# Later stage times for the first and last attention groups, and two-tile last parts in the out projections, in a two-layer trunk on one core

## The chip, the core and the metric

The kernel runs on one core of one Trainium2 chip. The time is what the device takes for one launch, in microseconds (us); every engine of the core works through its own queue in order, and semaphores hold an instruction until what it reads is written and what it overwrites has been read. Three runs of the kernel before took 843.97, 845.14 and 845.42 us, median 845.14.

## What is computed

The reference is a trunk of two layers over 256 positions of width 2048, in float32. Layer 0 is attention with a forgetting term (32 heads of 64), layer 1 sliding-window attention (32 query heads, 4 key heads, window 128) with sinks and a partial rotation. Both take one input projection that also gives a gate, and end with an output projection that is added to x.

```python
for i in range(DEPTH):
    h = rmsnorm(x, norm_g[i])
    if i % N_MIXERS == 0:
        p = h @ fox_w_in[j]                  # q, k, v, gate (2048 each), log_f (32)
        y = fox_attention(q, k, v, log_f)    # softmax(q k / 8 + c[t] - c[s], causal) v
        w_out = fox_w_out[j]
    else:
        p = h @ swa_w_in[j]                  # q 2048, k 256, v 256, gate 2048
        y = swa_attention(q, k, v, swa_sinks[j])
        w_out = swa_w_out[j]
    y = y * jax.nn.silu(gate)
    x = x + y @ w_out
return rmsnorm(x, final_g)
```

## The kernel before, in words

Each float32 operand of a product is split into a high half (a cast to the matrix engine's 32-bit format) and a low half (what the cast lost), so one product of the reference is three products on TensorE: high by high and high by low in one matmul with 512 columns, low by high in one with 256. Weights stream from memory. `load` (L189 to L209) issues a transfer on SyncE's queue into one of three `wraw` buffers, ScalarE casts the high half (L205), VectorE subtracts to get the low half (L206), both into one of five `w` buffers. In a trace or an order, `w_4453` is one such tile: the number only tells tiles apart.

A `Unit` is 256 columns of an output, two column blocks of 128 (c = 0 and 1). Its 2048 deep sum is 16 weight tiles, taken in parts; a part of four tiles is 8 matmuls for each column block. `block(unit, p, c)` (L211 to L249) issues those of one part and one column block into the accumulator `acc` of that column block, one of four PSUM buffers. The loop at L883 to L895 walks a list of parts, the stream, and issues the part's block for c = 0 and then the previous part's block for c = 1, so that a part's weights are fetched three parts ahead (LOOK). All matmuls run on TensorE in the order of the program.

The attention is cut into stages that are hung into this stream. A counter, the clock, makes one tick for every two matmuls, and `after(steps, fn)` (L103) runs fn that many ticks later. For each group of two column blocks of queries a table such as FOX_DUE holds two pairs of numbers and a single one: for head pair 0 and head pair 1, the tick of the first query-key product `s` (its second pair of matmuls comes SECOND = 8 ticks later) and the tick at which the probabilities are transposed and copied (`t`); the single number is the tick of the products with the values. They count from the end of the group's key projection (L499). In layer 0 a head pair's products go to two PSUM buffers `ps_s`; VectorE adds the bias (L350) and takes the maximum (L336), ScalarE makes the exponentials (L293), VectorE scales them (L304). The second pair of matmuls of `s` writes a buffer that L336 must have read. The gate of a group takes three steps on ScalarE (L263 to L265) and more on VectorE.

An output projection (`out_units`, L583) is eight units. When an accumulator is complete, its consumer copies one half of it on ScalarE (L253, `low_half`), and VectorE adds that copy (L587) and then the accumulator itself (L588) to x. Only after L588 is the accumulator free. The first two units of each out projection begin while the last group's attention is still running; the order of their parts is written out in `out_stream` (L839).

Of the kernel before, what the change touches and what calls it, by code (L numbers as in the profile page):

```python
# [37 lines left out]


FOX_DUE = ((16, 44), (48, 74), 106)  # L40
FOX_FIRST = ((46, 76), (80, 108), 122)
FOX_LAST = ((14, 40), (44, 72), 88)
SWA_DUE = ((16, 40), (44, 64), 74)
SWA_LAST = ((26, 45), (30, 56), 68)

SECOND = 8
WBUFS = 5
# [7 lines left out]
def trunk(  # L55
# [45 lines left out]
    due = {}  # L101
# [149 lines left out]
    def low_half(ps):  # L251
        s = work.tile([P, S], F32, tag="row", name="half", bufs=4)
        nc.scalar.copy(s, ps[:, S : 2 * S])  # L253
        return s

    def whole(src, kind, consume, **kw):
        return Unit([(src[q], [4, 4]) for q in range(2)], kind, consume, **kw)
# [59 lines left out]
    class Pair:  # L317
# [36 lines left out]
        def s_first(self):  # L354

            rng, qb = BLK[0]
            ps = ps_s.tile([P, 512], F32, tag="S", name="ps_s")
            ps = ps.rearrange("p (h a k) -> p h a k", h=2, k=P)
            for hh in range(2):
                self.product(ps[:, hh], hh, qb, P)  # L360
            nc.vector.tensor_add(self.st[:, :, rng], ps[:, :, 1, :], self.bias[:, :, rng])  # L361
            for hh in range(2):
                self.reduce(ps[:, hh, 0, :], hh, rng, qb)
            self.soft(self.st, self.mx)
# [73 lines left out]
    ones_row, z, a = (once[0:H, i * S : (i + 1) * S] for i in range(3))  # L438
# [33 lines left out]
    class FoxGroup(Group):  # L472
# [13 lines left out]
        def k(self, c, ps):  # L486
            t = fox.tile([P, S], F32, tag="k", name="k", bufs=2)
            nc.vector.tensor_add(t, ps[:, 0:S], low_half(ps))
            nc.vector.tensor_mul(t, t, r0()[:, 0:S])
            kk = fox.tile([P, 2, 2, S], F32R, tag="kk", name="kk", bufs=2)  # L490
            for hh, (w, other) in enumerate(((TOP, BOTTOM), (BOTTOM, TOP))):
                nc.scalar.copy(kk[w, hh, 0, :], t[w, :])
                nc.scalar.copy(kk[other, hh, 0, :], t[w, :])
                high = kk[w, hh, 0, :].bitcast(F32)
                nc.vector.tensor_sub(kk[w, hh, 1, :], t[w, :], high)
                nc.vector.tensor_sub(kk[other, hh, 1, :], t[w, :], high)  # L496
            self.kT[c] = kk
            if c == 0:
                due = {0: FOX_FIRST, 7: FOX_LAST}.get(self.g, FOX_DUE)  # L499
                self.attend(2 * self.g, due, False, False)  # L500

        def v(self, c, ps):
# [16 lines left out]
        def pair(self, j):  # L519
            h0 = 4 * self.g + 2 * j  # L520

            def bias():

                assert "forgot" in state
                bc = fox.tile([P, 2, 3 * P], F32, tag="bc", name="bc")
                nc.gpsimd.dma_start(out=bc, in_=negc_d[h0 : h0 + 2, :].partition_broadcast(P))  # L526
                for hh in range(2):
                    diagonal = bc[:, hh, :].rearrange("p (b k) -> p b k", k=P)[:, 0:3:2, :]
                    filled = fill_where_not(diagonal, [[0, 2], [-1, P]], 0, 1)
                if h0 == SINK:  # L530
                    with tc.issue_after(filled.ins):
                        nc.gpsimd.dma_start(out=state["sink"], in_=sink_d.partition_broadcast(P))
                return bc

            def soft(st, mx):

                c2 = cq[:, :, h0 : h0 + 2]
                nc.vector.tensor_add(mx, mx, c2)
                nc.vector.tensor_sub(mx, c2, mx)  # L539
                normalise(st, exps(st, mx))  # L540

            def operands():
                kk = self.kT[j]
                return self.qT[j], (kk[:, 0], kk[:, 1])

            return Pair(j, operands, 1.0, soft, bias)
# [36 lines left out]
    def out_units(src, done):  # L583
        def consumer(u):
            def consume(c, ps):
                m = 2 * u + c
                nc.vector.tensor_add(xT[:, m, :], low_half(ps), xT[:, m, :])  # L587
                nc.vector.tensor_add(xT[:, m, :], ps[:, 0:S], xT[:, m, :])  # L588
                done(m)

            return consume

        first = [
            Unit(
                [(src[u, 0], [4, 4]), (src[u, 1][:, 0:4, :], [4]), (src[u, 1][:, 4:8, :], [4])],
                "wgt", consumer(u), acts=ys,
            )
            for u in range(2)
        ]
        return first + [whole(src[u], "wgt", consumer(u), acts=ys) for u in range(2, 8)]  # L600
# [115 lines left out]

    fox_units = units
    first_out = out_units(fox_out_d, to_layer1)


# [32 lines left out]
    class SwaGroup(Group):  # L753
# [6 lines left out]
        def q(self, c, ps):  # L760
# [3 lines left out]
            if c == 0:  # L764
                self.attend(2 * self.u, SWA_LAST if self.u == 7 else SWA_DUE, self.u == 7, True)

# [27 lines left out]
    for u in range(8):  # L794
        G = SwaGroup(u)
        swa_units.append(whole(swa_in_d[u], "wgt", G.q))
        swa_units.append(whole(swa_in_d[10 + u], "wgt", gate_consumer(r1, G, u == 7)))

    last_out = out_units(swa_out_d, to_end)
    last_out[7] = whole(swa_out_d[7], "tok", finish, acts=ys, halves=False)  # L800

# [34 lines left out]
    def in_turn(units):  # L836
        return [(u, p) for u in units for p in range(len(u.parts))]

    def out_stream(units):  # L839

        a, b = units[0:2]
        early = [(a, 0), (a, 1), (a, 2), (b, 0), (b, 1), (b, 2), (a, 3), (b, 3)]
        return early + in_turn(units[2:])


# [3 lines left out]
    start += [(q0, 5), (v0, 6), (v0, 7), (k0, 5), (q0, 6), (v0, 8), (k0, 6)]  # L849
    stream = (  # L850
        start + in_turn(fox_units[3:]) + out_stream(first_out) + in_turn(swa_units) + out_stream(last_out)
    )
    fetched = [0]
# [107 lines left out]
```

## Time and profile before

| | us |
|---|---|
| three runs | 843.97, 845.14, 845.42 (median 845.14) |
| profiled execution | 844.52 |
| its span | 842.5 |
| TensorE busy | 828.4 |
| VectorE busy | 669.7 |
| ScalarE busy | 545.2 |
| mean granted TensorE clock | 0.995 of full |

The profile is one execution. Busy times are sums over the engine's instructions; TensorE's instructions are pipelined, so the distance between the starts of two rows says more of its speed than the length of a row. The granted clock is the share of full speed that the chip's control gave TensorE. A bracket at a row's end is the engine's idle time ahead of it, and who ended it.

### The profile page before, as it was taken

What the parts mean: (1) busy time and instruction counts of PE and PEld (TensorE: products, weight loads), DVE (VectorE), ACT (ScalarE), POOL (GpSimd) and SP (SyncE); (2) the same over time, 40 slices, a digit from 0 to 9 for tenths busy, and PEclk for the clock granted to TensorE, in tenths of its full rate; (3) what the DMA queues carried; (4) which work ended last, traced back from release to release, by engine and by line L of the source; (5) the groups of instructions that cost most, each with busy time, mean ns of one, the idle gap of its engine ahead of it and who ended that gap; (6) DMA issues with size and microseconds to landing.
All of it is one profiled execution on the core that took longest, in us unless ns stands there. A gap on an engine that the chain in (4) does not pass through costs nothing.

```text
span 842.5 us, 13416 instructions
## 1 busy us (share of the span) xinstructions
PE 828.4 (98%) x4906; PEld 717.1 (85%) x4906; DVE 669.7 (79%) x1428; ACT 545.2 (65%) x1067; POOL 61.6 (7%) x93
## 2 busy tenths in 40 slices
PE   8999999999999999999999999999999999999996
PEld 7887888888888888888888888888888888888885
DVE  5898978879687887968677778788898889876555
ACT  6676866757576675756555555567766776666552
POOL 1020100100000010000011110000000000003211
PEclk9999999999999999999999999999999999999998
DMA  8666554646455464654465554544444435354532
GB/s 280 235 237 210 172 195 158 231 156 212 171 178 209 156 232 155 204 179 137 175 208 193 200 187 163 180 170 129 171 151 151 158 144 166 134 196 164 197 100 100
DMA packets 26385, 150.51 MB, mean 179 GB/s; under 512 B 3232, under 2 KB 5440, under 8 KB 10704
## 3 DMA queue, kind: packets, MB, share of 16 engines
q1 hardware_dynamic: 23904, 142.22, 49.2%
q0 software_dynamic: 1408, 6.36, 2.4%
q10 hardware_dynamic: 1008, 1.07, 0.4%
q8 instruction: 39, 0.64, 0.3%
q14 instruction: 26, 0.21, 0.1%
HBM read 147.50 MB, written 2.15 MB: 178 GB/s over the span
## 4 chain that ended last, share of the span: by engine, by line
PE 88%; DVE 6%; DMA 2%; ACT 2%; issue 1%; SPq 1%; DVEq 0%; ACTq 0%
PE acc L76 79%; PE ps_s L76 3%; PE psy L76 3%; PE pt L79 2%; DVE w L206 2%; DMA wraw<-in_fox_in_dram 2%; DMA wraw<-in_vf_dram 1%; ACT w L205 0%; ACT st L293 0%; DVE ssq L824 0%; SPq L200 0%; DVE q L314 0%; DVE xs L157 0%; DVE st L397 0%; DVE kk L496 0%
## 5 line engine op out<-in xcount | busy, mean ns | idle before, releaser
L76 PE MATMUL acc<-xs,w 128*128 128x256 f32 (+1 forms) x2624 | 486.4, 340 | 0.3 <-ACT w L205 0.3
L76 PEld LDWEIGHTS acc<-xs,w 128*128 128x128 f32 x2624 | 407.6, 189 | 60.7 <-issue 3.9
L206 DVE TENSOR_TENSOR w<-wraw,w 128x1024 fp32r<-128x1024 f32 (+4 forms) x275 | 323.9, 1183 | 99.3 <-ACT w L205 97.1
L205 ACT CAST w<-wraw 128x1024 fp32r<-128x1024 f32 (+4 forms) x275 | 278.3, 1016 | 146.6 <-PE acc L76 124.7
L76 PE MATMUL acc<-ys,w 128*128 128x512 f32 x960 | 170.8, 338 | 0.0
L76 PEld LDWEIGHTS acc<-ys,w 128*128 128x128 f32 x960 | 147.6, 189 | 21.6 <-issue 0.6
L76 PE MATMUL acc<-w,xs 128*128 128x256 f32 (+2 forms) x608 | 114.3, 334 | 1.3 <-ACT w L205 0.7
L76 PEld LDWEIGHTS acc<-w,xs 128*128 128x128 f32 x608 | 94.6, 189 | 14.5 <-ACT w L205 1.8
L253 ACT COPY half<-acc 128x256 f32<-128x256 f32 x112 | 41.3, 369 | 52.1 <-PE acc L76 51.3
L293 ACT ACTIVATE st<-st,mx 128x128 f32<-128x128 f32 (+1 forms) x128 | 56.7, 444 | 11.5 <-DVE mx L539 5.7
L372 ACT COPY pts<-pt 128x384 f32<-128x384 f32 x64 | 30.4, 475 | 14.1 <-PE pt L79 14.1
L76 PE MATMUL ps_s<-kk,q 128*128 128x512 f32 (+2 forms) x192 | 35.9, 307 | 3.2 <-DVE mx L336 2.4
L610 POOL TENSOR_TENSOR acc<-acc,sq 128x256 f32<-128x256 f32 x28 | 29.9, 1069 | 105.1 <-ACT sq L604 105.1
L304 DVE TENSOR_SCALAR st<-st,rl 128x128 f32<-128x128 f32 (+1 forms) x128 | 33.3, 323 | 1.0
L79 PE MATMUL pt<-ident,st 128*128 128x128 f32 x192 | 31.4, 272 | 0.0
L76 PEld LDWEIGHTS ps_s<-kk,q 128*128 128x128 f32 x192 | 26.3, 190 | 5.1 <-issue 3.6
L608 POOL COPY acc<-sq 128x256 f32<-128x256 f32 x2 | 1.9, 936 | 327.0 <-ACT sq L604 327.0
L79 PEld LDWEIGHTS pt<-ident,st 128*128 128x128 f32 x192 | 23.3, 140 | 2.5
L526 POOL DMA_DIRECT2D bc<-negc_d x16 | 8.8, 553 | 219.3 <-DVE st L361 188.3
L313 ACT CAST q<-qT 64x256 fp32r<-64x256 f32 x32 | 12.8, 401 | 18.6 <-DVE qT L734 18.2
L157 DVE SCALAR_TENSOR_TENSOR xs<-xT,g_sb,xs 128x256 fp32r<-128x256 f32 x32 | 22.0, 711 | 3.2 <-ACT xs L156 3.2
L293 ACT ACTIVATION_READ_ACCUMULATOR st<-st,mx 128x1 f32 x128 | 23.9, 187 | 0.0
(136 smaller groups left out, 590.6 us busy)
## 6 DMA issues: line engine op xcount, KB each, us to landing
wraw<-in_fox_in_dram SPq DMA_DIRECT2D x58, 1024.0 KB, 5.0
wraw<-in_swa_in_dram SPq DMA_DIRECT2D x36, 1024.0 KB, 4.9
wraw<-in_fox_out_dram SPq DMA_DIRECT2D x14, 1024.0 KB, 5.0
wraw<-in_swa_out_dram SPq DMA_DIRECT2D x14, 1024.0 KB, 4.9
bc<-negc_d POOLq DMA_DIRECT2D x16, 384.0 KB, 4.9
wraw<-in_fox_in_dram SPq DMA_DIRECT2D x4, 512.0 KB, 5.6
wraw<-in_fox_out_dram SPq DMA_DIRECT2D x4, 512.0 KB, 3.7
wraw<-in_swa_out_dram SPq DMA_DIRECT2D x4, 512.0 KB, 3.7
```

Source lines behind the costliest of these rows:

```text
L76: tc.keep_in_program_order(nc.tensor.matmul(*args, **kw))
L79: tc.keep_in_program_order(nc.tensor.transpose(out, in_, ident))
L157: nc.vector.scalar_tensor_tensor(out=xs[:, kt, 1, :], in0=xT[:, kt, :], scalar=g, in1=xs[:, kt, 0, :].bitcast(F32), op0=ALU.mult, op1=ALU. ...
L205: state["split"] = nc.scalar.copy(w[:, :, 0, :], raw)
L206: nc.vector.tensor_tensor(out=w[:, :, 1, :], in0=raw, in1=w[:, :, 0, :].bitcast(F32), op=ALU.subtract)
L253: nc.scalar.copy(s, ps[:, S : 2 * S])
L293: nc.scalar.activation(st[:, hh, rng], st[:, hh, rng], AF.Exp, bias=nm[:, qb, hh : hh + 1], accum_out=l[:, qb, hh : hh + 1],)
L304: nc.vector.tensor_scalar_mul(st[:, hh, rng], st[:, hh, rng], rl[:, qb, hh : hh + 1])
L313: nc.scalar.copy(q2[w, hh, :], t[w, :])
L372: nc.scalar.copy(group.pts[hh][:, self.j, :], pt[:, 0 : 3 * P])
L526: nc.gpsimd.dma_start(out=bc, in_=negc_d[h0 : h0 + 2, :].partition_broadcast(P))
L610: nc.gpsimd.tensor_add(sums[0], sums[0], s)
```

## The change

Group 0's stages of layer 0 (FOX_FIRST) all come 8 ticks later. Group 1 gets a table of its own, in which the first head pair comes 6 ticks later and the second 6 ticks later too, with the products with the values at the same tick. The last group of layer 0 (FOX_LAST) and of layer 1 (SWA_LAST) come 0 to 4 ticks later, the latter's first `s` at the same tick. In both out projections the first two units' parts are cut otherwise: eight tiles, four, two and two instead of eight, four and four, with the second transfer holding 6 tiles and the third 2; and the order of these two units' parts is a0 to a3, b0 to b3, a4, b4 instead of a0, a1, a2, b0, b1, b2, a3, b3.

```diff
 FOX_DUE = ((16, 44), (48, 74), 106)
-FOX_FIRST = ((46, 76), (80, 108), 122)
-FOX_LAST = ((14, 40), (44, 72), 88)
+FOX_FIRST = ((54, 84), (88, 116), 130)
+FOX_NEXT = ((22, 50), (54, 80), 106)
+FOX_LAST = ((16, 44), (48, 76), 92)
 SWA_DUE = ((16, 40), (44, 64), 74)
-SWA_LAST = ((26, 45), (30, 56), 68)
+SWA_LAST = ((26, 48), (34, 60), 72)
...
-                due = {0: FOX_FIRST, 7: FOX_LAST}.get(self.g, FOX_DUE)
+                due = {0: FOX_FIRST, 1: FOX_NEXT, 7: FOX_LAST}.get(self.g, FOX_DUE)
...
         first = [
             Unit(
-                [(src[u, 0], [4, 4]), (src[u, 1][:, 0:4, :], [4]), (src[u, 1][:, 4:8, :], [4])],
+                [(src[u, 0], [4, 4]), (src[u, 1][:, 0:6, :], [4, 2]), (src[u, 1][:, 6:8, :], [2])],
                 "wgt", consumer(u), acts=ys,
             )
             for u in range(2)
...
         a, b = units[0:2]
-        early = [(a, 0), (a, 1), (a, 2), (b, 0), (b, 1), (b, 2), (a, 3), (b, 3)]
+        early = [(u, p) for u in (a, b) for p in range(4)] + [(a, 4), (b, 4)]
         return early + in_turn(units[2:])
```

The changed file has one line more near its top, so its line numbers are one higher: the subtraction is L207, the bias addition L351, the maximum L337, the accumulator's addition L589.

The first place is VectorE at group 0's first query-key product, in the order before:

```order
L206 TENSOR_TENSOR w_743<-wraw_741,w_743 128x4x256
L350 TENSOR_TENSOR st_754<-ps_s_756,bc_698 128x256
L350 TENSOR_TENSOR st_754<-ps_s_757,bc_698 128x256
L336 ISA st_754,mx_755<-ps_s_756,st_754 128x256
L336 ISA mx_755 128x1
```

The same place in the changed kernel:

```order
L207 TENSOR_TENSOR w_743<-wraw_741,w_743 128x4x256
L207 TENSOR_TENSOR w_763<-wraw_741,w_763 128x4x256
L351 TENSOR_TENSOR st_774<-ps_s_776,bc_718 128x256
L351 TENSOR_TENSOR st_774<-ps_s_777,bc_718 128x256
L337 ISA st_774,mx_775<-ps_s_776,st_774 128x256
L337 ISA mx_775 128x1
```

A second weight subtraction, of w_763, now stands ahead of the two bias additions; before, the subtraction of that weight tile stood behind the maximum.

The second place is VectorE in layer 0's out projection, where the first unit (its accumulator for c = 0 is acc_4338 before) is consumed. Before:

```order
L206 TENSOR_TENSOR w_4466<-wraw_4464,w_4466 128x4x256
L206 TENSOR_TENSOR w_4485<-wraw_4464,w_4485 128x4x256
L587 TENSOR_TENSOR xT_82<-half_4496,xT_82 128x256
L588 TENSOR_TENSOR xT_82<-acc_4338,xT_82 128x256
L206 TENSOR_TENSOR w_4516<-wraw_4514,w_4516 128x4x256
L157 SCALAR_TENSOR_TENSOR xs_80<-xT_82,g_sb_58,xs_80 128x256
```

In the changed kernel, where that accumulator is acc_4336:

```order
L207 TENSOR_TENSOR w_4496<-wraw_4494,w_4496 128x4x256
L207 TENSOR_TENSOR w_4511<-wraw_4494,w_4511 128x4x256
L588 TENSOR_TENSOR xT_82<-half_4518,xT_82 128x256
L207 TENSOR_TENSOR w_4534<-wraw_4532,w_4534 128x4x256
L589 TENSOR_TENSOR xT_82<-acc_4336,xT_82 128x256
L207 TENSOR_TENSOR w_4563<-wraw_4532,w_4563 128x4x256
```

A weight subtraction, of w_4534, now stands between the addition of the copied half and that of the accumulator. The order in layer 1's out projection differs in the same way.

The third place is TensorE there, from the first unit's last block for c = 0 (acc_4338 and w_4422 before) to the third unit's first (acc_4556 before). Before:

```order
L76 MATMUL acc_4338<-ys_81,w_4422 128x512 x4
L76 MATMUL acc_4338<-ys_81,w_4422 128x256 x4
L76 MATMUL acc_4455<-ys_81,w_4389 128x512 x4
L76 MATMUL acc_4455<-ys_81,w_4389 128x256 x4
L76 MATMUL acc_4425<-ys_81,w_4444 128x512 x4
L76 MATMUL acc_4425<-ys_81,w_4444 128x256 x4
L76 MATMUL acc_4378<-ys_81,w_4422 128x512 x4
L76 MATMUL acc_4378<-ys_81,w_4422 128x256 x4
L76 MATMUL acc_4556<-ys_81,w_4466 128x512 x4
```

And in the changed kernel, from acc_4336 and w_4453 to acc_4566:

```order
L77 MATMUL acc_4464<-ys_81,w_4420 128x512 x4
L77 MATMUL acc_4464<-ys_81,w_4420 128x256 x4
L77 MATMUL acc_4336<-ys_81,w_4453 128x512 x2
L77 MATMUL acc_4336<-ys_81,w_4453 128x256 x2
L77 MATMUL acc_4464<-ys_81,w_4435 128x512 x2
L77 MATMUL acc_4464<-ys_81,w_4435 128x256 x2
L77 MATMUL acc_4438<-ys_81,w_4475 128x512 x2
L77 MATMUL acc_4438<-ys_81,w_4475 128x256 x2
L77 MATMUL acc_4378<-ys_81,w_4453 128x512 x2
L77 MATMUL acc_4378<-ys_81,w_4453 128x256 x2
L77 MATMUL acc_4566<-ys_81,w_4496 128x512 x4
```

Between the two stand 16 matmuls, counting the first unit's last block, where there were 32. The third unit's first accumulator takes the buffer of the first unit's for c = 0 in both kernels.

## The prediction

> **What bounds the kernel now.** I read the page first, then TensorE's waits, then the timeline of the places where it waits. The profiled execution took 844.52 us, 842.5 of them the span; the sum below is made against it. The page's first part and its chain of waits:
>
> ```profile
> PE 828.4 (98%) x4906; PEld 717.1 (85%) x4906; DVE 669.7 (79%) x1428; ACT 545.2 (65%) x1067; POOL 61.6 (7%) x93
> PE 88%; DVE 6%; DMA 2%; ACT 2%; issue 1%; SPq 1%; DVEq 0%; ACTq 0%
> ```
>
> TensorE is busy for 98% of the span and 88% of the chain is its own work. The number of products hardly depends on the change, so what it can bring or cost is TensorE's idle time, and the clock that idle time takes with it. TensorE's waits, grouped by who releases them (total us, count, longest):
>
> ```profile
> PE ps_s L76 <- DVE mx L336: 2.4, 1, 2.4
> PE acc L76 <- ACT w L205: 1.0, 2, 0.7
> PE ps_s L76 <- DVE kk L496: 0.6, 2, 0.4
> ```
>
> One wait of 2.4 us for VectorE stands out, and two small ones for the keys (`kk`). TensorE's timeline around them (start, us, operation, count, idle before it):
>
> ```profile
> 59.33 0.62 PE L76 MATMUL ps_s<-kk,q 128*128 128x512 f32 x2
> 59.79 2.94 PE L76 MATMUL acc<-xs,w 128*128 128x512 f32 x16
> 65.18 0.47 PE L76 MATMUL ps_s<-kk,q 128*128 128x256 f32 x2 [2.44 <-DVE mx L336]
> 65.49 9.63 PE L76 MATMUL acc<-xs,w 128*128 128x512 f32 x44
> 74.95 0.49 PE L79 MATMUL pt<-ident,st 128*128 128x128 f32 x3
> ...
> 80.51 7.18 PE L76 MATMUL acc<-xs,w 128*128 128x256 f32 x40
> 87.52 0.49 PE L79 MATMUL pt<-ident,st 128*128 128x128 f32 x3
> ...
> 88.33 0.40 PE L76 MATMUL ps_s<-kk,q 128*128 128x512 f32 x1
> 89.11 0.47 PE L76 MATMUL ps_s<-kk,q 128*128 128x512 f32 x1 [0.39 <-DVE kk L496]
> ```
>
> From these I take my unit: 40 products from 80.51 to 87.52 are 7.01 us, 0.1753 us each, so 16 of them (a part of four tiles, both column blocks) are 2.81 us. By that, 44 products should take 7.71 us, but from 65.49 to 74.95 they took 9.46: 1.75 us more, with no wait in them. The windows of half a microsecond say why (after the busy times, the granted clock, then DMA share and GB/s):
>
> ```profile
> 66.00:66.50 0.50, 0.50 (x3) 0.45 (x2) 0.50 (x2) 0.49 (x1) 0.00 (x0) 0.66 0.33 115
> 69.00:69.50 0.50, 0.50 (x3) 0.40 (x3) 0.50 (x1) 0.00 (x0) 0.00 (x0) 0.50 0.58 111
> 69.50:70.00 0.50, 0.50 (x5) 0.50 (x5) 0.50 (x2) 0.00 (x0) 0.00 (x0) 0.93 0.74 180
> ```
>
> The granted clock falls to 0.50 at about 66.16 (0.66 is the mean of 0.16 us at full and 0.34 at half) and is back at about 69.53: 3.4 us at half speed, 1.7 us lost. So the wait of 2.44 us cost 2.6 us of start-to-start time (62.60, where the 16 products end by my unit, to 65.18) and 1.7 us behind it.
>
> **The change, part by part.** First, group 0's stages come 8 ticks, 16 products, later. The first product (`ps_s`, two matmuls) is hung behind the 16 products that it stood ahead of; behind it come 16 others, then the pair that waits. Everything up to the pair is the same work: 59.33 + 2.81 + 0.46 (the pair's 59.33 to 59.79) + 2.81 = 65.41. VectorE's and ScalarE's rows decide whether the pair can run then:
>
> ```profile
> 62.60 1.42 DVE L206 TENSOR_TENSOR w<-wraw,w 128x1024 fp32r<-128x1024 f32 x1
> 63.95 0.74 DVE L350 TENSOR_TENSOR st<-ps_s,bc 128x256 f32<-128x256 f32 x2
> 64.61 0.41 DVE L336 CUSTOM_DVE_ANT_0 st<-ps_s,st 128x256 f32<-128x256 f32 x1
> 68.79 1.22 DVE L206 TENSOR_TENSOR w<-wraw,w 128x1024 fp32r<-128x1024 f32 x1 [0.25 <-ACT w L205]
> 69.93 0.15 DVE L539 TENSOR_TENSOR mx<-cq,mx 128x4 f32<-128x4 f32 x1
> ```
>
> ```profile
> 63.38 0.63 ACT L264 ACTIVATE gate_e<-gate_e 128x512 f32<-128x512 f32 x1
> 64.04 0.63 ACT L265 ACTIVATE gate_e<-gate_e 128x512 f32<-128x512 f32 x1
> 64.58 1.03 ACT L205 CAST w<-wraw 128x1024 fp32r<-128x1024 f32 x1
> 67.71 1.04 ACT L205 CAST w<-wraw 128x1024 fp32r<-128x1024 f32 x1 [1.07 <-PE acc L76]
> ```
>
> Later on TensorE is not simply later on VectorE: in the new order a second weight subtraction (w_763) stands ahead of the two bias additions (L350) on VectorE's queue, and its cast stands ahead of one gate step on ScalarE. The cast can start at 63.38 + 0.54 (64.04 to 64.58) = 63.92; the subtraction follows 1.08 later (67.71 to 68.79), at 65.00; the next operation 1.14 later (68.79 to 69.93), at 66.14; from the first addition to TensorE's pair are 1.23 us (63.95 to 65.18): 67.37. The pair then waits 67.37 − 65.41 = **1.96 us instead of 2.58: −0.62 us**. The wait moves with its cause. Were the subtraction not in between, the whole 2.58 would go; that is the other end. On the losing side I find nothing above the old price, since what was queued there is the same work.
>
> The clock behind it is the open price: 1.7 us if 1.96 us of idleness still lowers it, nothing if not. The trace has a fall after 2.44 us and none after the 0.78 us start-to-start at 88.33. 1.96 is nearer to 2.44; I take **no gain, 0**, with −1.7 as the other end.
>
> [...]
>
> Second, group 1's stages come 6 ticks later. At 88.33 to 89.11 its keys were late: 0.78 where a pair's first takes 0.23 (half of 0.46), 0.55 lost. 12 products more (2.1 us) ahead of it cover that, **−0.55**. Against it stands that TensorE, less held up, arrives earlier: 0.62 at most, still covered; with the dip gone too it comes 2.3 us earlier and some 0.35 remains. For the following stages of the two groups the same chaining leaves 0 to 0.5 us between what TensorE wants and what VectorE has ready, so 0, with +0.5 as the worse end.
>
> Third, the layers' last groups, 2 to 4 ticks later:
>
> ```profile
> 386.15 0.40 PE L76 MATMUL ps_s<-kk,q 128*128 128x512 f32 x1
> 386.77 0.47 PE L76 MATMUL ps_s<-kk,q 128*128 128x512 f32 x1 [0.23 <-DVE kk L496]
> ```
>
> ```profile
> 732.89 1.09 PE L76 MATMUL ps_s<-kk,q 128*128 128x128 f32 x8
> 733.82 1.57 PE L76 MATMUL acc<-xs,w 128*128 128x256 f32 x8
> 735.39 1.49 PE L76 MATMUL ps_s<-kk,q 128*128 128x128 f32 x8
> 736.72 2.04 PE L76 MATMUL acc<-xs,w 128*128 128x256 f32 x12
> ```
>
> In layer 0 the second product comes 0.62 after the first, 0.39 of it lost; the row names 0.23 as idle. I take 0.3. In layer 1 eight products took 1.33 us (735.39 to 736.72) where the same eight took 0.93 (732.89 to 733.82): 0.40. Both are covered by 4 to 8 products more: **−0.3 and −0.40**.
>
> Fourth, the out projections. Two more casts and subtractions of half size each cost nothing as long as both engines wait there, and they do (1.77 us before a cast, 1.59 before a subtraction, next fence). The two weight transfers become 768 and 256 KB instead of twice 512, in the same queue and three parts ahead: 0. The products are the same, only four last blocks are now two tiles long. That makes the distance short between the first unit's last block and the third unit's first, which takes over the first unit's accumulator. The rows, TensorE's lag to ScalarE at layer 0's end first:
>
> ```profile
> 409.01 1.64 PE L76 MATMUL acc<-w,xs 128*128 128x512 f32 x8
> 416.62 3.77 PE L76 MATMUL acc<-ys,w 128*128 128x512 f32 x19
> ```
>
> ```profile
> 409.30 0.48 ACT L372 COPY pts<-pt 128x384 f32<-128x384 f32 x1 [0.29 <-PE pt L79]
> 426.79 1.05 ACT L205 CAST w<-wraw 128x1024 fp32r<-128x1024 f32 x1 [1.77 <-PE acc L76]
> ```
>
> ```profile
> 427.88 1.23 DVE L206 TENSOR_TENSOR w<-wraw,w 128x1024 fp32r<-128x1024 f32 x1 [1.59 <-ACT w L205]
> 429.02 0.42 DVE L587 TENSOR_TENSOR xT<-half,xT 128x256 f32<-128x256 f32 x1
> ...
> 435.97 0.42 DVE L588 TENSOR_TENSOR xT<-acc,xT 128x256 f32<-128x256 f32 x1
> 436.31 1.22 DVE L206 TENSOR_TENSOR w<-wraw,w 128x1024 fp32r<-128x1024 f32 x1
> ```
>
> Let T be the start of the first unit's last block (w_4453). TensorE wants the third unit's first product (acc_4566) four blocks of four products later: T + 16 × 0.1753 = T + 2.80. That product waits for VectorE's addition of acc_4336 (L588 of before). At T the buffer of w_4420 comes free; the cast of w_4511 into it starts at T + 0.29 (the block at 409.01, the copy at 409.30), its subtraction 1.09 later (426.79 to 427.88) at 1.38, the half's addition 1.14 later at 2.52. Next on VectorE's queue is now not the accumulator's addition but the subtraction of w_4534, at 2.52 + 0.34 (435.97 to 436.31) = 2.86; its cast, freed at T + 1.40 by the block of w_4435, is ready for that, 1.40 + 0.29 + 1.09 = 2.78. The accumulator's addition starts 1.14 later, T + 4.00, ends after 0.42 at 4.42, and TensorE follows 0.16 later (65.02, the end of the L336 row, to 65.18): T + 4.58. **The new wait is 4.58 − 2.80 = 1.78 us.** Before, these four blocks were four tiles long, TensorE wanted the accumulator at T + 5.61 and no wait shows. Behind the waiting product stands everything: all matmuls run in program order. Layer 1's end has the same order on VectorE, so **+3.56** together. The ends: 1.65 if the links are 0.13 shorter together, 1.85 if the cast of w_4534 is 0.15 later than worked out; and 1.7 more for each that lowers the clock, as 2.44 us did; 1.78 is a little nearer to that than to 0.78, but 0.66 short of it, and I take none.
>
> **Sum.** 844.52 + 3.56 − 0.62 − 0.55 − 0.3 − 0.40 = 846.2 us against the profiled execution. The median of the three runs, 845.14, is 0.62 above that execution; I give half of it and forecast **846.5 us**.
>
> **The rivals.**
> *New clock falls.* The 1.78-us waits lower the clock, once or in both layers: 846.2 + 1.7 = 847.9, or 849.6. [...]
> *No fall at all.* Waits of below 2 us leave the clock alone, the old fall goes: start −2.3 (0.62 + 1.7) and 0.2 of the keys' wait instead of 0.55: 844.52 + 3.56 − 2.32 − 0.2 − 0.7 = 844.9, no change. For it: the shorter gaps of the trace left the clock at full. Against: 1.96 is 80% of 2.44. [...]
> *The out projection does not wait.* If the addition of acc_4336 ran ahead of w_4534's subtraction, or VectorE were 1.8 us earlier than my chain, only the gains stay: 844.52 − 1.87 = 842.6, and 841.0 without the fall: faster. For it: TensorE shows no wait over the whole out projection today, and VectorE idles 1.59 us there. Against: the order of VectorE's queue is fixed, and each link of the chain has its row.
>
> **How the numbers follow.** Forecast .40, new falls .27, no fall .16, no new wait .17. Changes below 0.2% (1.7 us: 843.45 to 846.83) can't be told from none here. Of the forecast, with its own spread of about 1 us and its median between 846.2 and 846.8, .25 lies within and .15 above; new falls lie above, .27; no fall lies within, .16; no new wait lies below with .15, and .02 within. So faster .15, same .43, slower .42. The range reaches down to 843.2, which leaves most of the third rival out, and up to 849.4, which leaves the double fall's upper half out. The likeliest case's own range is 845.2 to 847.4.
>
> **What would show it.** Each out projection has one wait of 1.6 to 1.9 us on `acc`, released by VectorE's accumulator addition, some 2.8 us behind the start of the first unit's last block; if none is there, the fourth part is wrong. The wait at 65 is still on the VectorE maximum (L336 of before), near 2 us, at about 65.4, with a weight subtraction just ahead of the bias additions; if it is under 0.5, my queue reading there is wrong. The windows behind all three waits show whether the clock fell: that is the price I know least. The keys' waits at 89 and 387 and the long eight products at 735 should be gone.

## The result

The changed kernel takes 846.65 us (median of 20 runs, 845.33 to 848.13), the kernel before 844.41 (20 runs, 842.98 to 845.97): a ratio of 1.0025, with a 95% interval of 1.0018 to 1.0032. So it is slower by 2.2 us, and 0.15 us off the forecast. The interval excludes no change at all; its lower end, 0.18%, just reaches below the 0.2% that the prediction takes as the least that can be told from none. The profiled execution took 845.78 us, with a span of 843.8.

TensorE's waits in the changed kernel (total us, count, longest) show the price at once:

```profile
PE acc L77 <- DVE xT L589: 3.1, 2, 1.6
PE ps_s L77 <- DVE mx L337: 1.7, 1, 1.7
...
PE pt L80 <- DVE st L305: 0.7, 1, 0.7
PE ps_s L77 <- DVE kk L497: 0.4, 1, 0.4
```

The first row is new: twice 1.57 us for VectorE's addition of an accumulator. TensorE's and VectorE's timelines at the first of the two, and ScalarE's cast of w_4511:

```profile
416.35 14.95 PE L77 MATMUL acc<-ys,w 128*128 128x512 f32 x84
432.86 12.40 PE L77 MATMUL acc<-ys,w 128*128 128x512 f32 x69 [1.57 <-DVE xT L589]
```

```profile
429.68 1.23 DVE L207 TENSOR_TENSOR w<-wraw,w 128x1024 fp32r<-128x1024 f32 x1 [0.88 <-ACT w L206]
430.82 0.42 DVE L588 TENSOR_TENSOR xT<-half,xT 128x256 f32<-128x256 f32 x1
431.16 1.22 DVE L207 TENSOR_TENSOR w<-wraw,w 128x1024 fp32r<-128x1024 f32 x1
432.29 0.42 DVE L589 TENSOR_TENSOR xT<-acc,xT 128x256 f32<-128x256 f32 x1
```

```profile
428.60 1.05 ACT L206 CAST w<-wraw 128x1024 fp32r<-128x1024 f32 x1 [1.06 <-PE acc L77]
```

With T = 428.60 − 0.29 = 428.31 the subtraction starts at T + 1.37, the half's addition at T + 2.51, the subtraction between the two at T + 2.85, the accumulator's addition at T + 3.98, TensorE at T + 4.55. It wanted the accumulator at T + 2.80 = 431.11; counted on TensorE alone, the 84 products that start at 416.35 end at 431.08, so T is right. From start to start the wait costs 1.75 us.

The start of the changed kernel, on TensorE:

```profile
62.56 2.95 PE L77 MATMUL acc<-xs,w 128*128 128x512 f32 x16
67.20 0.47 PE L77 MATMUL ps_s<-kk,q 128*128 128x256 f32 x2 [1.68 <-DVE mx L337]
67.51 8.09 PE L77 MATMUL acc<-xs,w 128*128 128x512 f32 x44
75.44 0.49 PE L80 MATMUL pt<-ident,st 128*128 128x128 f32 x3
...
88.28 0.48 PE L77 MATMUL ps_s<-kk,q 128*128 128x512 f32 x1
89.17 0.47 PE L77 MATMUL ps_s<-kk,q 128*128 128x512 f32 x1 [0.41 <-DVE kk L497]
...
111.74 1.56 PE L77 MATMUL acc<-xs,w 128*128 128x512 f32 x8
114.01 0.70 PE L80 MATMUL pt<-ident,st 128*128 128x128 f32 x3 [0.70 <-DVE st L305]
```

The wait for the maximum is 1.68 us (1.83 from start to start: 67.20 − 62.56 − 2.81). VectorE shows the second weight subtraction ahead of the bias additions, 0.18 us earlier than forecast:

```profile
64.82 1.23 DVE L207 TENSOR_TENSOR w<-wraw,w 128x1024 fp32r<-128x1024 f32 x1 [1.17 <-ACT w L206]
65.96 0.74 DVE L351 TENSOR_TENSOR st<-ps_s,bc 128x256 f32<-128x256 f32 x2
```

In this execution the clock did not fall behind it: the 44 products took 7.93 us instead of 9.46. The wait for the keys at 88 is still there, and a new one stands before the transposes at 114.

To see what each stretch gave, I compare the products with the values (`psy`), which stand once in every group. Of before, and then of the change:

```profile
125.55 1.57 PE L76 MATMUL psy<-pts,vg 128*64 128x256 f32 x16
371.93 1.57 PE L76 MATMUL psy<-pts,vg 128*64 128x256 f32 x16
415.11 1.57 PE L76 MATMUL psy<-pts,vg 128*64 128x256 f32 x16
562.53 1.52 PE L76 MATMUL psy<-pts,vs 128*64 128x512 f32 x8
751.21 1.52 PE L76 MATMUL psy<-pts,vs 128*64 128x512 f32 x8
```

```profile
124.30 1.57 PE L77 MATMUL psy<-pts,vg 128*64 128x256 f32 x16
370.72 1.57 PE L77 MATMUL psy<-pts,vg 128*64 128x256 f32 x16
414.84 1.57 PE L77 MATMUL psy<-pts,vg 128*64 128x256 f32 x16
562.61 1.52 PE L77 MATMUL psy<-pts,vs 128*64 128x512 f32 x8
752.10 1.52 PE L77 MATMUL psy<-pts,vs 128*64 128x512 f32 x8
```

By the second group the changed kernel is 1.25 us ahead, and between there and 371 nothing happens. (That 1.25 us is mostly the fall of the clock that this execution didn't have; the run of the last groups alone shows it.) At 415 and 752 the products are hung 4 ticks later than before, behind 8 products (1.40 us) more, which have to be taken off: the last group of layer 0 gained 0.46 us (−0.27 − 1.40 = −1.67 after −1.21), the out projection of layer 0 lost 1.75 (from −1.67 to +0.08), layer 1's last group gained some 0.6 (0.89 − 1.40 = −0.51 after +0.08), and the rest, to the span's +1.3, is the second out projection's loss of 1.8.

### The profile page after: what moved, and what is told of

It is laid out like the page before. It is cut to its first block, busy times and chain, and to the rows that moved or that the text cites. A ratio compares the mean times of both kernels' runs of the same rounds, so it can differ in the third digit from the quotient of the medians.

```text
span 843.8 us, 13420 instructions
## 1 busy us (share of the span) xinstructions
PE 827.5 (98%) x4906; PEld 717.1 (85%) x4906; DVE 668.6 (79%) x1432; ACT 546.2 (65%) x1071; POOL 59.9 (7%) x93
## 4 chain that ended last, share of the span: by engine, by line
PE 88%; DVE 5%; ACT 2%; DMA 2%; issue 2%; SPq 1%; DVEq 0%; ACTq 0%
PE acc L77 79%; PE ps_s L77 3%; PE psy L77 3%; PE pt L80 2%; DVE w L207 2%; DMA wraw<-in_fox_in_dram 2%; ACT w L206 1%; SPq L201 1%; ACT st L294 0%; DVE ssq L825 0%; DVE xs L158 0%; SPq L813 0%; DVE q L315 0%; DVE scaled L705 0%; DVE kk L497 0%
## 5 line engine op out<-in xcount | busy, mean ns | idle before, releaser
L207 DVE TENSOR_TENSOR w<-wraw,w 128x1024 fp32r<-128x1024 f32 (+4 forms) x279 | 324.5, 1166 | 100.7 <-ACT w L206 98.3
L77 PE MATMUL acc<-ys,w 128*128 128x512 f32 (+1 forms) x960 | 171.4, 338 | 3.1 <-DVE xT L589 3.1
L294 ACT ACTIVATE st<-st,mx 128x128 f32<-128x128 f32 (+1 forms) x128 | 56.7, 444 | 12.7 <-DVE mx L540 7.2
L294 ACT ACTIVATION_READ_ACCUMULATOR st<-st,mx 128x1 f32 x128 | 23.9, 187 | 0.0
```

Source lines behind the costliest of these rows:

```text
L77: tc.keep_in_program_order(nc.tensor.matmul(*args, **kw))
L207: nc.vector.tensor_tensor(out=w[:, :, 1, :], in0=raw, in1=w[:, :, 0, :].bitcast(F32), op=ALU.subtract)
L294: nc.scalar.activation(st[:, hh, rng], st[:, hh, rng], AF.Exp, bias=nm[:, qb, hh : hh + 1], accum_out=l[:, qb, hh : hh + 1],)
```

## The experiments

In these, line numbers are those of each run's own file and differ by one or two, and each median stands beside that of the kernel before on the same chip. Many runs share one reading, the mean granted clock of an execution: 3.4 us at half speed, as in the profile of before, are 1.7 us of 843, or 0.002 of that mean. It is a rough sign. The traces of the kernel before and of the changed one also have the clock at half in their last 4.9 and 3.9 us, where TensorE has run out of work, and that takes another 0.003 and 0.002 off the mean. In the kernel before (us, then busy times, the granted clock at 0.50, DMA share and GB/s):

```profile
838.00:840.00 2.00, 0.00 (x0) 0.00 (x0) 1.18 (x3) 0.00 (x0) 0.00 (x0) 0.50 0.92 330
```

Of the profiled executions, the two with a fall in the trace (before, and the later stage times with the out projections as before) have a mean of 0.995, the others 0.996 to 0.998. So I take a mean of 0.995 or less as a sign of a fall ahead of the end, 0.997 and more as a sign of none, and 0.996 as either; that is an estimate, and counts by 0.995 can miss some.

**One part at a time: the start alone.**

```diff
-FOX_FIRST = ((46, 76), (80, 108), 122)
+FOX_FIRST = ((54, 84), (88, 116), 130)
+FOX_NEXT = ((22, 50), (54, 80), 106)
...
-                due = {0: FOX_FIRST, 7: FOX_LAST}.get(self.g, FOX_DUE)
+                due = {0: FOX_FIRST, 1: FOX_NEXT, 7: FOX_LAST}.get(self.g, FOX_DUE)
```

> Only the stage tables of the first two groups are changed, the rest is the kernel before. My theory: the pair's wait in group 0 stays, 1.7 us idle instead of 2.4, the clock does not fall behind it, and half of that gain is given back by 115 us because VectorE is behind (a new wait of some 0.7 us before a transpose near 114): the second product with the values starts some 1.2 us earlier than in the kernel before, and the time is 1.2 us lower, 843.2 against a median of 844.4. Rival: the whole of the removed wait and clock fall stays gained, 842.1 or less. Second rival: the gain was that one execution's, whose clock did not fall by chance, and the time is that of before.

Measured: 843.42 us against 844.08, a ratio of 0.9992 (0.9983 to 1.0000). That is 0.66 us, about half of what my theory said, and the interval reaches the second rival's no change. In the trace the second `psy` stands 1.2 us earlier than before, with the wait at 114 (0.7 us) in it. But before's profiled execution had a fall of the clock and this one hadn't. Of 11 executions 1 has a mean clock of 0.995 or less; of the kernel before's, over the four comparisons, 48 of 86. Its eight executions at 0.997 and above take 843.07 to 844.12, with a median of 843.4; the eight of the kernel before at that clock on the same chip have 843.4 too. So what the start's new times gained is, by this count, fewer executions with a fall; between executions without one there is next to no gain.

**The last groups alone.**

```diff
-FOX_LAST = ((14, 40), (44, 72), 88)
+FOX_LAST = ((16, 44), (48, 76), 92)
...
-SWA_LAST = ((26, 45), (30, 56), 68)
+SWA_LAST = ((26, 48), (34, 60), 72)
```

> Only the last groups' stages are later, the rest is the kernel before. My theory: 0.5 to 0.6 us less in each layer, 844.1 - 1.0 = 843.1; the wait for the keys near 387 and the long eight products near 735 are gone. Rival: what is gained there is lost again behind it in the out projection, and the time is that of before.

Measured: 843.41 against 844.44, 0.9986 (0.9977 to 0.9995). The theory holds: 1.03 us, and none of it is given back. The two places that the prediction named are mended in the changed kernel's trace as well: no wait for the keys near 387, and the eight products from 736.70 take 0.92 us instead of 1.33.

This run's profiled execution has the old start, with a wait of 2.2 us, and no fall behind it. Its second `psy`:

```profile
124.17 1.57 PE L76 MATMUL psy<-pts,vg 128*64 128x256 f32 x16
```

That is as early as in the changed kernel (124.30). To take out what happened ahead of the attention, count from group 0's first query-key product. It starts at 59.05 here, at 59.33 in the kernel before, and in the changed kernel, 2.81 us of products later, at 62.09. The second `psy` follows after 65.12, 66.22 and 62.21 + 2.81 = 65.02 us. So against an old start without a fall the changed start gains 0.1 us; the 1.2 us against the profile of before are its fall, of whose 1.53 us (9.46 against 7.93 for the 44 products) 1.1 are left by then.

**The out projections alone.**

```diff
-                [(src[u, 0], [4, 4]), (src[u, 1][:, 0:4, :], [4]), (src[u, 1][:, 4:8, :], [4])],
+                [(src[u, 0], [4, 4]), (src[u, 1][:, 0:6, :], [4, 2]), (src[u, 1][:, 6:8, :], [2])],
...
-        early = [(a, 0), (a, 1), (a, 2), (b, 0), (b, 1), (b, 2), (a, 3), (b, 3)]
+        early = [(u, p) for u in (a, b) for p in range(4)] + [(a, 4), (b, 4)]
```

> Only the out projections' first units are cut and ordered as in the change. My theory: one wait of 1.5 to 1.6 us idle (1.75 from start to start) on the accumulator's addition in each layer and nothing else: 844.4 + 3.5 = 847.9, more where the clock falls behind them. Rival: part of the changed kernel's loss came from its last groups' stages, then this one is less than 2 us slower than the kernel before.

Measured: 847.81 against 844.08, 1.0039 (1.0027 to 1.0051), with the two waits of 1.57 us. The three parts add up: −0.66 − 1.03 + 3.73 = +2.04, against +2.24 for the whole. This run's trace held a surprise at the old start:

```profile
65.11 0.48 PE L76 MATMUL ps_s<-kk,q 128*128 128x256 f32 x2 [2.49 <-DVE mx L336]
65.42 8.09 PE L76 MATMUL acc<-xs,w 128*128 128x512 f32 x44
73.35 0.49 PE L79 MATMUL pt<-ident,st 128*128 128x128 f32 x3
```

The same wait as before, even 0.05 us longer, and the 44 products behind it take 7.93 us: no fall.

**The accumulator's wait taken away.** The third unit accumulates in the scores' two PSUM buffers, which are idle by then:

```diff
-        return first + [whole(src[u], "wgt", consumer(u), acts=ys) for u in range(2, 8)]
+        return first + [
+            whole(src[u], "wgt", consumer(u), acts=ys, acc=(ps_s, "S") if u == 2 else None)
+            for u in range(2, 8)
+        ]
```

> The changed kernel, with the third unit of each out projection accumulating in the two PSUM buffers of the scores, which are idle there, so that it does not wait for the first unit's accumulators. My theory: both waits of 1.57 us go, 1.75 us each from start to start, and no other takes their place: 846.65 - 3.5 = 843.1 us, faster than the kernel before. Rival: the weights are the cause (half-size casts and subtractions, other transfers), the waits only move to the weights of the third unit and the time stays at 846 to 847.

Measured: 843.45 against 844.08, 0.9991 (0.9982 to 0.9999), and TensorE waits for no addition in the trace. The theory holds; weights, transfers and half-size casts are not the cause. The traces say so without the spread of the times: from the `psy` at 415 to the one at 562 TensorE takes 145.96 us here, 147.77 in the changed kernel, and 145.96 in the run further below that has the same stage times and the old out projections. From the `psy` at 751 to the kernel's last products (`rows`) it is 83.75, 85.56 and 83.80. The two waits, 1.8 us each by this measure, are the whole price of the new cut.

**The two additions exchanged.**

```diff
-                nc.vector.tensor_add(xT[:, m, :], low_half(ps), xT[:, m, :])
+                half = low_half(ps)
                 nc.vector.tensor_add(xT[:, m, :], ps[:, 0:S], xT[:, m, :])
+                nc.vector.tensor_add(xT[:, m, :], half, xT[:, m, :])
```

> The changed kernel, with the two additions of an out projection's consumer in the other order: the accumulator first, the copied half second. The accumulator then comes free ahead of the weight subtraction between them, 1.14 + 0.34 us earlier. My theory: the waits go from 1.75 to 0.3 us each, 846.65 - 2.9 = 843.7 us. Rival: the accumulator's addition is held by something else than the place in VectorE's queue, and the wait stays over 1 us.

Measured: 843.15 against 844.08, 0.9992 (0.9983 to 1.0000). TensorE's row in layer 0's out projection:

```profile
415.80 24.37 PE L77 MATMUL acc<-ys,w 128*128 128x512 f32 x136
```

136 products in one row; at 0.1753 us each they are 23.84, so half a us at most is left for a wait; by the two distances used above (146.11 and 84.04 us) 0.15 and 0.24 are left, as expected. VectorE's order was the cause: with the same additions, but the accumulator's one ahead of the subtraction, the time is 3.5 us below the changed kernel's, 3.2 when each is set against the kernel before of its own comparison.

**One size changed: last parts of three tiles.**

```diff
-                [(src[u, 0], [4, 4]), (src[u, 1][:, 0:6, :], [4, 2]), (src[u, 1][:, 6:8, :], [2])],
+                [(src[u, 0], [4, 4]), (src[u, 1][:, 0:5, :], [4, 1]), (src[u, 1][:, 5:8, :], [3])],
```

> The changed kernel with the two units' last parts three tiles long instead of two (8, 4, 1 and 3 tiles). My theory: the distance from the first unit's last block to the third unit's first product is 24 products instead of 16, 4.21 us instead of 2.80, and VectorE's chain stays at 4.55: the waits go from 1.75 to some 0.35 us each, 846.65 - 2.8 = 843.9. Rival: the wait comes with the order of the parts, whatever their length, and stays over 1 us.

Measured: 844.87 against 844.44, 1.0009 (1.0000 to 1.0018), waits of 0.8 us where I expected 0.35.

```profile
433.19 17.17 PE L77 MATMUL acc<-ys,w 128*128 128x512 f32 x96 [0.83 <-DVE xT L589]
```

```profile
430.01 1.23 DVE L207 TENSOR_TENSOR w<-wraw,w 128x1024 fp32r<-128x1024 f32 x1 [0.55 <-ACT w L206]
432.63 0.42 DVE L589 TENSOR_TENSOR xT<-acc,xT 128x256 f32<-128x256 f32 x1
```

The chain is the forecast's, T + 4.55 (433.19, with T = 430.01 − 1.37 = 428.64). My count of the distance was wrong: the second unit's part between them is now one tile long, so the four blocks hold 6 + 2 + 6 + 6 = 20 products, not 24. TensorE wants the accumulator at T + 3.51, and 4.55 − 3.51 = 1.04 us from start to start is what stands there. So the wait follows the distance.

**The good parts together: later stage times, out projections as before.**

> All of the change's later stage times (first two groups and the layers' last groups), with the out projections as before. My theory: the parts add up. The last groups gave 0.46 us in layer 0 and 0.58 in layer 1 by the distances in the changed kernel, the start alone 843.4: so 842.4 us, no wait on the accumulator, faster than before by 0.2%. Rival: the last groups' stages, hung later, need the out projections' new cut to have work beside them; then a new wait stands at 409 or 747 and the time is 843.4 or more.

Measured: 842.53 against 844.44, 0.9980 (0.9971 to 0.9989), as expected, and faster than before. Its profiled execution had a fall of the clock behind a wait of only 1.85 us:

```profile
67.27 0.48 PE L77 MATMUL ps_s<-kk,q 128*128 128x256 f32 x2 [1.85 <-DVE mx L337]
67.59 9.65 PE L77 MATMUL acc<-xs,w 128*128 128x512 f32 x44
77.07 0.49 PE L80 MATMUL pt<-ident,st 128*128 128x128 f32 x3
```

```profile
66.00:68.00 2.00, 0.73 (x4) 0.66 (x5) 2.00 (x9) 0.33 (x1) 0.00 (x0) 0.90 0.63 127
68.00:70.00 2.00, 2.00 (x8) 1.71 (x7) 2.00 (x4) 0.89 (x2) 0.00 (x0) 0.50 0.92 385
70.00:72.00 2.00, 2.00 (x11) 1.73 (x11) 1.54 (x8) 1.05 (x1) 0.55 (x1) 0.74 0.41 156
```

**The start's wait covered.** By now I held that VectorE is behind until 115 us, whatever is hung where. To test it, 20 more products were put ahead of the waiting pair (on top of the last kernel):

```diff
-FOX_FIRST = ((54, 84), (88, 116), 130)
+FOX_FIRST = ((54, 94), (88, 116), 130)
...
-            after(SECOND, self.s_first)
+            after(self.second, self.s_first)
...
+            self.second = 18 if self.j == 0 and getattr(group, "g", None) == 0 else SECOND
```

> Later stage times as in the run with those alone, out projections as before, and for group 0's first head pair the second pair of matmuls hung 18 ticks behind the first instead of 8, its transposes 10 ticks later: 20 products more stand ahead of the pair that waits. My theory: VectorE is behind until some 115 us, so the 1.7-us wait at 65 goes and most of it comes back as waits near 75 to 115 on the maximum, the keys or the scaled probabilities; the second product with the values starts within 0.7 us of where it does without this, 842.4 to 841.7 us. Rival: the wait is local, all of it is gained, 840.7 us.

Measured: 842.09 against 844.44, 0.9975 (0.9966 to 0.9985), 0.44 us less than without it, which is within the intervals. TensorE at the places that wait:

```profile
79.78 0.47 PE L77 MATMUL ps_s<-kk,q 128*128 128x256 f32 x2 [0.96 <-DVE mx L337]
...
88.57 0.47 PE L77 MATMUL ps_s<-kk,q 128*128 128x512 f32 x1 [0.42 <-ACT w L206]
...
113.96 0.70 PE L80 MATMUL pt<-ident,st 128*128 128x128 f32 x3 [1.08 <-DVE st L305]
```

The wait of 1.85 us at 65 is gone. Those at 80 and 88 have come instead, and the one at 114 has grown from 0.70 to 1.08. The transposes start at 113.96, in the changed kernel at 114.01. That is what the theory says; but it is also what one late chain before those transposes would do.

**That chain's wait covered.** What is late there shows in VectorE's order of before, and then of the change, at group 1's second head pair:

```profile
109.36 0.17 DVE L538 TENSOR_TENSOR mx<-mx,cq 128x4 f32<-128x4 f32 x1
109.56 0.16 DVE L539 TENSOR_TENSOR mx<-cq,mx 128x4 f32<-128x4 f32 x1
109.74 1.23 DVE L206 TENSOR_TENSOR w<-wraw,w 128x1024 fp32r<-128x1024 f32 x1
```

```profile
110.08 0.15 DVE L539 TENSOR_TENSOR mx<-mx,cq 128x4 f32<-128x4 f32 x1
110.22 1.23 DVE L207 TENSOR_TENSOR w<-wraw,w 128x1024 fp32r<-128x1024 f32 x1
111.36 0.16 DVE L540 TENSOR_TENSOR mx<-cq,mx 128x4 f32<-128x4 f32 x1
```

A weight subtraction has slipped between two steps of 0.15 us, and the exponentials behind them start 1.8 us later (ScalarE's L294 at 111.56; L293 of before at 109.76): 1.14 for the subtraction, the rest because the first step itself stands later. Hanging the transposes 12 products later covers that; first without the edit of the last run, then with it:

```diff
-FOX_NEXT = ((22, 50), (54, 80), 106)
+FOX_NEXT = ((22, 50), (54, 86), 106)
```

> Later stage times with the out projections as before, and group 1's second head pair transposed 6 ticks (12 products, 2.1 us) later: 86 instead of 80. In the changed kernel a weight subtraction stands on VectorE between the two small steps on the maximum ahead of that pair's exponentials, which start at 111.56 instead of 109.76, and TensorE waits 0.7 us before the transposes at 114. My theory: that wait goes, 0.87 us from start to start, nothing takes its place: 842.5 - 0.85 = 841.7. Rival: VectorE is behind in its sum of work, and the wait comes back at the next product or transpose: 842.5.

> As the run with group 0's second pair of matmuls 18 ticks behind the first, and group 1's second head pair transposed 6 ticks later. My theory: the wait of 1.1 us at 114 goes, the one of 1.0 at 80 and the short one at 88 stay: 842.1 - 1.2 = 840.9. Rival, VectorE behind in its sum of work: 842.1, with the wait at another place.

Measured: 841.43 and 840.25 us, against 844.34: ratios of 0.9977 (0.9965 to 0.9989) and 0.9958 (0.9944 to 0.9972). In neither is there a wait at 114. My reading that VectorE is behind in its sum of work falls: the 1.2 us between these two runs is what covering the wait at 65 brings once the wait at 114 no longer swallows it; with that wait in place the same edit brought 0.44. The intervals of the two runs overlap by a little, but the traces agree: from the first query-key product to the second `psy` they take 61.53 and 60.43 us.

**The next wait covered too.**

```diff
-FOX_FIRST = ((54, 94), (88, 116), 130)
+FOX_FIRST = ((54, 94), (88, 122), 134)
...
-            self.second = 18 if self.j == 0 and getattr(group, "g", None) == 0 else SECOND
+            self.second = (18, 14)[self.j] if getattr(group, "g", None) == 0 else SECOND
```

> As the last one, and in group 0's second head pair too the second pair of matmuls is hung later, 14 ticks behind the first, with its transposes 6 and the products with the values 4 ticks later. My theory: the wait at 80 (0.96 idle, 1.2 from start to start) goes, but VectorE still sets when group 1's keys are ready (88.5 in every run so far), so most of it moves to the wait there: 840.9 to 840.2. Rival: all of it is gained, 839.7 and less.

Measured: 839.73 against 844.34, 0.9952 (0.9940 to 0.9965), the fastest of all, 4.6 us less than before and 6.9 less than the changed kernel. Its waits at the keys and the maximum:

```profile
PE ps_s L77 <- DVE mx L337: 0.5, 1, 0.5
PE ps_s L77 <- DVE kk L498: 0.3, 1, 0.3
```

And its product that waits for the keys:

```profile
86.59 0.47 PE L77 MATMUL ps_s<-kk,q 128*128 128x512 f32 x1 [0.30 <-DVE kk L498]
```

It starts 2 us earlier than in the run before the transposes were hung later (88.57), 1.6 when both are counted from their first query-key product, so that time was no constant of VectorE's either. My theory's 840.2 to 840.9 is missed and the rival's 839.7 met, but both were counted from 840.9. From the 840.25 that the run before really took, 0.5 of the 1.2 us is gained, and a wait of 0.5 us on the maximum has come up at 90.81. So a part did move on, though not to the keys.

**Do the out projections' waits lower the clock?** Their new cut, put on the fastest kernel:

> The fastest of the runs so far, in which no wait of the start is over 0.5 us, with the change's cut and order of the out projections put back. Its only waits over 1 us ahead of the tail are then the two on the accumulators. My theory: 1.57 us of idleness are short of what lowers the clock; 839.7 + 3.5 = 843.2 us, and every run has the mean granted clock of 0.997 to 0.998 that it has without. Rival: these waits, too, lower the clock in some executions; then some runs show 0.996 or 0.995 and 1.7 or 3.4 us more.

Measured: 843.88 against 844.45, 0.9993 (0.9984 to 1.0002), 11 executions between 843.4 and 844.65. The two waits:

```profile
431.00 4.20 PE L77 MATMUL acc<-ys,w 128*128 128x512 f32 x22 [1.75 <-DVE xT L590]
...
764.00 26.19 PE L77 MATMUL acc<-ys,w 128*128 128x512 f32 x148 [1.57 <-DVE xT L590]
```

No execution has a mean clock below 0.996, and the highest time is 1.25 us above the lowest: in 22 such waits I see no fall, though only two of them stand in a trace (the clock there is 1.00 from 425 to 437 and from 760 to 768 us) and a mean of 0.996, which three executions have, doesn't exclude one by itself. The cut costs 4.15 us here (4.04 against the kernel before of each comparison) where 3.5 were expected. By the two distances used above, the out projections take 2.14 and 1.76 us longer than in the fastest kernel, 3.9 together: the first wait is 0.18 longer than in the changed kernel, and without the cut the fastest kernel's first out projection is 0.15 shorter than that of the later stage times alone. The rest lies within the spread of the runs.

## Why the prediction was right

| step | forecast | measured |
|---|---|---|
| pair at 65, from start to start | −0.62 | −0.75 (1.83 instead of 2.58) |
| clock behind it | 0 (other end −1.7) | −1.53 in the two profiled executions, one with a fall, one without |
| keys at 88 | −0.55 | +0.11 (0.66 lost instead of 0.55) |
| other stages of the first groups | 0 (worse end +0.5) | +0.87, the wait at 114 |
| last groups | −0.7 | −0.46 and −0.6 by the traces, −1.03 by their own run |
| out projections | +3.56 | +1.75 and +1.8 by the traces, +3.73 by their own run |
| from the profiled execution to the median | +0.31 | +0.87 |

**The out projections** came out link by link: each of VectorE's starts within 0.03 us of its place, the release at T + 4.55 instead of 4.58. This is the step that decided the sign, and three runs show its cause: another accumulator or another order of two additions takes the wait away, and another distance changes it as counted. The rival without a new wait is out.

**The start** has the right sum, −1.17 against −1.25, by luck: the profile of before had a fall and that of the change had none. Against the two traces with the old start and no fall, the changed kernel's gain is 0.1 to 0.3 us. The pair's wait did shrink by what VectorE's queue gave. The keys' term failed: I took it that TensorE would come late enough, as it does in the one trace with the new start and a fall; without a fall I had 0.2 to 0.35 left, and 0.66 is there. And the step "0 to 0.5 us between what TensorE wants and what VectorE has ready, so 0" failed at 114, for the very reason that I had found in the out projections: the new order puts a subtraction inside a short chain. I had looked for that at two places of the queue and not at a third. The two profiled executions differ by a fall, so +1.26 us between them understates +2.24 between the medians, in which about half of before's executions have no fall either.

**The number** is closer than the working. The sum, 846.2, is 0.4 above the changed kernel's profiled execution, and the median stands 0.87 above that execution where I had added 0.31. That 0.31 came from three runs; with 20 the median of the kernel before is 0.11 below its profiled execution. The two misses cancel, and a range 6 us wide would have held most of the rivals too. What lifts the median is not settled. Nine executions take 845.3 to 846.0 us and eleven 846.6 to 848.1; only four of these eleven have a mean clock of 0.995, and the other seven, at 0.996 to 0.998, show no clear fall. Something ahead of the attention may do it: among the traces with the new start and no edit to it, group 0's first query-key product starts anywhere from 61.7 to 63.5 us.

**The clock** was wrongly asked. I weighed which length of wait lowers it, and set 1.96 us from start to start against 2.44 us of idleness, two unlike measures; in the runs the length alone did not decide it. The rival with new falls has the last run against it, for waits of 1.6 to 1.75 us there. The one with no fall at all describes the profiled execution (845.78, of which 0.87 is the wait at 114 that it did not have); without the four executions at a mean clock of 0.995, whose median is 847.7, the median is 845.9. But its condition, that waits of below 2 us leave the clock alone, does not hold: behind 1.85 us it fell in the profile of the later stage times with the out projections as before. One and the same wait had a fall in one execution and none in another (2.44 us in the profile of before, 2.49 with the out projections alone).

## What to carry to other kernels

When stages are hung later, look in the other engines' order at every short chain that TensorE waits for, not only at the one that is meant: a bulk operation that slipped between two of its steps held up all behind it by its whole length (1.14 us here). A wait swallowed the gains made ahead of it (0.44 us left with the wait at 114, 1.2 without it), so an edit that brings little may be worth its full price once the next wait is gone; try it again then. And before a last block is made shorter, count the products up to the next use of its accumulator against the consumer's chain, or let the consumer read the accumulator first.

## What the runs showed of the hardware

Behind the start's wait the granted clock fell to 0.50 in some executions of a kernel and, by the mean clock, not in others. By executions with a mean clock of 0.995 or less: where the start's wait in the trace is 2.2 to 2.5 us, 57 of 102 (before, the last groups alone, the out projections alone); where it is 1.2 to 1.9, 17 of 83 (the changed kernel and the runs with its start, with or without its out projections, and with the transposes later; single kernels range from 0 of 7 to 5 of 12); where no wait of the start exceeds 1.1 us, 0 of 30 (the four kernels with 20 products more ahead of it). Both falls that the traces show at the start last 3.4 us, after waits of 2.44 and 1.85 us; after 2.49 (the out projections alone), 2.21 (the last groups alone) and 1.90 us (the transposes later) the traces show none. With a fall the 44 products behind the wait took 9.46 and 9.48 us, without one 7.93 in the changed kernel. Of these 1.53 us, 0.9 to 1.1 were left at the second group of the kernel before (66.22 us from the first query-key product to the second `psy`, 65.12 and 65.32 in the two runs with the old start and no fall); much of the rest is taken up by the waits for the keys at 87 to 89, 0.84 and 0.71 us in those two runs against 0.39. So a shorter wait at the start brought two things: fewer executions at 0.995 or less, and its own length where no later wait swallowed it, as the 1.2 us of the transposes' two runs, which have no sign of a fall on either side. One execution of the three-tile run has a mean clock of 0.992 and one of the kernel before 0.993, which is further below 1 than one fall and the end (0.002 and 0.002 to 0.003) account for; no trace shows them.
